# Mean over the rows of an 8192x8192 matrix: four row groups loaded in pairs instead of one by one

## The chip, the cores and the metric

The kernel runs on one core of a Trainium2 chip. The metric is the device time in microseconds, the median over runs; lower is better. The engines that matter here are VectorE (DVE in the profile), TensorE (PE, with PEld for its weight loads), ScalarE (ACT), GpSimd (POOL) and SyncE (SP), which issues the transfers.

## The reference

```python
"x": np.random.randn(8192, 8192).astype(np.float32)

def reference(x):
    return np.mean(x, axis=0)
```

The input is 268.4 MB of float32 in device memory, the output 8192 sums over 8192 rows each, divided by 8192. Every element has to be read once.

## The kernel before

The rows are cut into G = 64 groups of P = 128 rows, one row for each partition. A group is 8192 columns wide, 4 MB, which the kernel counts as 16 blocks of F = 512 columns. The buffer `bufs` holds U = 6 such groups: slots 0 to 3 take the loads, slot 4 is called `both` and slot 5 `acc`, the running sum. The sum over the 128 partitions is made at the end by TensorE, with a column of 1/8192 (`ones`) as the stationary operand. Because a matmul with `ones` can also take a loaded group directly, the last groups are not all added by VectorE.

**The start.** Two small parts of later groups go to a tile of their own (`early`): the last two blocks of group 60, and blocks 9 to 13 of group 63. Groups 0 to 3 come as one load, 4 and 5 as another, and three adds of VectorE make the first `acc` of them.

**The loop of pairs** (line 120), for g = 6, 8, ... 54. One load brings two groups into two neighbouring slots (0 and 1, or 2 and 3, in turn); a partition gets two adjacent rows, 64 KB in one piece. VectorE first adds the two slots into `both`, then adds `both` to `acc`. The slots are free for the next load after the first of the two adds. In two rounds GpSimd adds a part of `early` to `acc` besides.

**The loop of single groups** (line 135), for g = 56 to 59. One load brings one group into one slot, 32 KB for each partition, and VectorE adds the slot to `acc`. The slots are, in this order, 2, 3, 0 and 1.

**The end** (lines 139 to 180). Group 60 comes without its last two blocks, and blocks 0 to 13 of it are added to `acc`. Group 61 comes whole, and VectorE adds blocks 7 to 15 of it to `acc`; TensorE takes blocks 0 to 6 from the buffer. Group 62 is read by TensorE from the buffer, but for blocks 14, 15 and 8, which GpSimd adds to `acc` (line 148). Group 63 comes in four pieces: blocks 4 to 7, 0 to 3, 14 and 15, and 8. Each of these loads goes to the slot of one of the groups 56 to 59: 60 to that of 56, 61 to that of 57, 62 to that of 58 and 63 to that of 59.

**Order and queues.** SyncE issues all loads, in program order. A load waits for the add that frees its slot; at every second load SyncE also waits for two loads that lie six to eight back (`load`, line 75). An add of VectorE that needs a fresh load waits for one no-op, on ScalarE or GpSimd, which in turn waits for that load and for the add before (`add`, line 94). Other adds follow the one before.

**TensorE's order** is written out by hand in the list `sums` (lines 167 to 181), and TensorE keeps to it. Each entry becomes two matmuls in the profile. The sums go to four PSUM tiles: `banks` for blocks 0 to 7, `wide` for 9 to 13, `two` for 14 and 15, `last` for 8. The first entries are blocks 2 to 4 and 0 and 1 of `acc`, blocks 0 to 6 of group 61, blocks 5 to 7 of `acc` and all of group 62's first eight; the last ones belong to the last piece of group 63. ScalarE copies `banks`, `wide` and `two` out of PSUM (line 198), VectorE copies `last` (line 214), and five stores write the output (line 201).

```python
    blocks(acc, 2, 5)
    blocks(acc, 0, 2)
    blocks(r61, 0, 7)
    blocks(acc, 5, 8)
    blocks(r62, 0, 8)
    ...
    spread(two, r63, 14, 16)
    spread(last, r63, 8, 9)
```

Of the kernel before, what the change touches and what calls it, by code (L numbers as in the profile page):

```python
# [9 lines left out]
def kernel(  # L10
# [2 lines left out]
    x: bass.AP,  # L13
    out: bass.AP,
):

    nc = tc.nc
    f32 = mybir.dt.float32
    M, N = x.shape  # L40
# [3 lines left out]
    G = M // P  # L44
# [6 lines left out]
    bufs = sb.tile([P, U, N], f32, name="bufs")  # L51
    both = bufs[:, U - 2, :]
    acc = bufs[:, U - 1, :]
# [21 lines left out]
    def load(dst, src):  # L75
        ins = tc.keep_in_program_order(nc.sync.dma_start(out=dst, in_=src)).ins  # L76
        k = len(loads)
        over = loads[k - 8:k - 6] if k >= 8 and k % 2 == 0 else []
        tc.declare_no_dep(ins, group="loads", keep=over, reason="the reader of the buffer waited")
        for o in over:  # L80
            tc.add_manual_dep(ins, o.name, sync, reason="covers the next load too")
        tc.add_to_no_dep_group("loads", ins)
        loads.append(ins)
        return ins

    def rows(g, n=1):
        return x[g * P:(g + n) * P, :]

    def load_rows(g, u, n):
        return load(bufs[:, u:u + n, :], rows(g, n).rearrange("(p j) c -> p j c", j=n))  # L90
# [3 lines left out]
    def add(dst, a, b, dmas):  # L94

        ins = nc.vector.tensor_add(out=dst, in0=a, in1=b).ins  # L96
        if dmas and adds:
            waiter = nc.scalar if len(adds) % 8 > 1 else nc.gpsimd
            nop = joins[waiter] = tc.keep_in_program_order(waiter.nop()).ins  # L99
            for o in dmas + adds[-1:]:  # L100
                tc.add_manual_dep(nop, o.name, sync, reason="the no-op waits")
            for group in ("loads", "adds"):
                tc.declare_no_dep(ins, group=group, reason="the no-op waited")
            tc.add_manual_dep(ins, nop.name, sync, reason="waits for both at once")
        elif adds:
            tc.declare_no_dep(ins, group="loads", reason="the add ahead waited")
        tc.declare_no_dep(ins, group="early", reason="the no-op waited, or the add behind it")
        tc.add_to_no_dep_group("adds", ins)
        adds.append(ins)
# [7 lines left out]
    tc.keep_in_program_order(nc.scalar.copy(out=warm[:], in_=ones[:]))  # L117
    ahead = []
    g = 6
    while g < G - 8:  # L120
        u = (g + 2) % 4
        dma = load_rows(g, u, 2)
        add(both, bufs[:, u, :], bufs[:, u + 1, :], [dma])
        add(acc, acc, both, ahead)
        ahead = []
        if g in (24, 32):
            lo, hi = (0, 4) if g == 24 else (4, 7)
            cols = slice((9 + lo) * F, (9 + hi) * F)
            ins = tc.keep_in_program_order(nc.gpsimd.tensor_add(  # L129
                out=acc[:, cols], in0=acc[:, cols], in1=early[:, lo * F:hi * F])).ins  # L130
            tc.add_to_no_dep_group("early", ins)
            ahead = [ins]
        g += 2

    while g < G - 4:
        row = bufs[:, (g + 2) % 4, :]
        add(acc, acc, row, [load(row, rows(g))])
        g += 1
    for lo, hi, loaded in [(0, 14, 14), (7, 16, 16)]:
        row = bufs[:, (g + 2) % 4, :]  # L140
        dma = load(row[:, :loaded * F], rows(g)[:, :loaded * F])
# [115 lines left out]
```

## Time and profile before

| | |
|---|---|
| time, median of 3 runs | 628.53 us (628.39 to 628.57) |
| span of the profiled execution | 626.4 us; the page gives no other time for it (the median is 2.13 us longer than this span) |
| VectorE busy | 529.3 us (85% of the span), 60 instructions |
| TensorE busy | 13.3 us (2%), 126 matmuls |
| GpSimd, ScalarE busy | 12.0 us, 3.7 us |
| read from memory | 268.44 MB, 429 GB/s over the span |
| an add of 128x8192 on VectorE | 8763 ns mean of 55; 482.0 us in all |
| VectorE's copy at the end | starts at 623.73 us |

All positions are microseconds from the start of the span. In a line of the timeline the first number is the start and the second the length of a run of like instructions; the bracket at its end says how long the engine was idle before and what released it. In the chain of waits each line is a start, a length and what the time went to. In a group of instructions, the numbers after the bar are busy time, mean ns of one, and the idle time before. In the rows of 40 digits, each digit is the busy share of one fortieth of the span in tenths.

### The profile page before, as it was taken

The numbers are of one execution on the slowest core, as the hardware profiler recorded it, in microseconds if no ns is written. First come the engines' busy times: TensorE is split into PE (matmuls) and PEld (weight loads), VectorE is DVE, ScalarE is ACT, GpSimd is POOL, SyncE is SP. The second block draws the span as 40 slices with busy tenths as digits, with TensorE's granted clock in tenths as the row PEclk, the third lists the DMA queues.
The fourth block names the chain that finished last, engine by engine and source line by source line (L and its number), as shares of the span: only waits on it lengthen the run. The fifth ranks groups of instructions, "written<-read, shape, count | busy, mean of one in ns | idle before, by whom it ended". The sixth has DMA issues, their size and how long they took to land.

```text
span 626.4 us, 484 instructions
## 1 busy us (share of the span) xinstructions
PE 13.3 (2%) x126; PEld 4.0 (1%) x126; DVE 529.3 (85%) x60; ACT 3.7 (1%) x6; POOL 12.0 (2%) x10
## 2 busy tenths in 40 slices
PE   0000000000000000000000000000000000000008
PEld 0000000000000000000000000000000000000002
DVE  0028999998888998889998899888898888999992
ACT  0000000000000000000000000000000000000001
POOL 0000000000000000020000200000000000000002
PEclk9999999999999999999999999999999999999999
DMA  8999999999999999999999999999999999999997
GB/s 372 465 402 428 459 410 460 402 469 402 469 402 469 402 469 402 469 402 469 402 465 406 439 431 427 444 410 460 402 469 402 469 402 469 402 435 435 419 435 305
DMA packets 5930, 268.50 MB, mean 429 GB/s; under 512 B 660, under 2 KB 668, under 8 KB 1064
## 3 DMA queue, kind: packets, MB, share of 16 engines
q1 hardware_dynamic: 5912, 268.46, 99.3%
q8 instruction: 1, 0.02, 0.0%
q10 hardware_dynamic: 16, 0.01, 0.0%
q14 instruction: 1, 0.01, 0.0%
HBM read 268.44 MB, written 0.03 MB: 429 GB/s over the span
## 4 chain that ended last, share of the span: by engine, by line
DMA 59%; DVE 30%; another core or an unknown queue 10%; issue 0%; SPq 0%; ACTq 0%; PE 0%; POOL 0%; POOLq 0%
DMA bufs<-in_x_dram 59%; DVE bufs L96 30%; SPq L76 0%; ACTq L99 0%; PE last L183 0%; DVE tail L214 0%; POOL ready L61 0%; POOL ones L58 0%; POOLq L99 0%; POOLq L241 0%
## 5 line engine op out<-in xcount | busy, mean ns | idle before, releaser
L96 DVE TENSOR_TENSOR bufs<-bufs 128x8192 f32<-128x8192 f32 (+3 forms) x59 | 529.0, 8966 | 85.9 <-DMA bufs<-in_x_dram 43.0
L183 PE MATMUL bank<-bufs,ones 128*32 128x512 f32 x62 | 10.0, 716 | 610.3 <-DVE bufs L96 610.0
L129 POOL TENSOR_TENSOR bufs<-bufs,early 128x2048 f32<-128x2048 f32 (+1 forms) x2 | 7.9, 3954 | 348.5 <-DVE bufs L96 348.5
L148 POOL TENSOR_TENSOR bufs<-bufs 128x1024 f32<-128x1024 f32 (+1 forms) x2 | 3.6, 1824 | 258.9 <-DMA bufs<-in_x_dram 258.9
L214 DVE COPY tail<-last 128x128 f32<-128x128 f32 x1 | 0.3, 291 | 8.8 <-PE last L183 8.8
L183 PEld LDWEIGHTS bank<-bufs,ones 128*32 128x32 f32 x62 | 2.2, 121 | 616.4 <-issue 614.5
L198 ACT COPY bufs<-bank 128x512 f32<-128x512 f32 x2 | 1.2, 586 | 617.9 <-PE bank L183 617.9
L183 PE MATMUL wide<-bufs,ones 128*32 128x512 f32 (+1 forms) x32 | 2.5, 432 | 0.0
L117 ACT ACT_TABLE_LOAD x1 | 1.3, 1283 | 0.7 <-PEq L241 0.7
L183 PE MATMUL two<-bufs,ones 128*32 128x256 f32 x16 | 1.2, 380 | 0.0
L183 PEld LDWEIGHTS wide<-bufs,ones 128*32 128x32 f32 x32 | 1.0, 110 | 1.8 <-issue 1.8
L183 PE MATMUL last<-bufs,ones 128*32 128x128 f32 x16 | 0.8, 279 | 0.1
L198 ACT COPY bufs<-wide 128x640 f32<-128x640 f32 x1 | 0.7, 692 | 1.1 <-PE wide L183 1.1
L183 PEld LDWEIGHTS last<-bufs,ones 128*32 128x32 f32 x16 | 0.4, 109 | 1.2 <-issue 0.6
L183 PEld LDWEIGHTS two<-bufs,ones 128*32 128x32 f32 x16 | 0.4, 109 | 0.1
L198 ACT COPY bufs<-two 128x256 f32<-128x256 f32 x1 | 0.4, 372 | 0.1
L117 ACT COPY warm<-ones 128x32 f32<-128x32 f32 x1 | 0.2, 217 | 0.0
L61 POOL TENSOR_TENSOR ready<-ones 128x1 f32<-128x1 f32 x1 | 0.2, 193 | 0.1
L58 POOL MEMSET ones<- 128x32 f32 x1 | 0.1, 125 | 0.3 <-POOLq L241 0.3
L241 POOL MEMSET const-float32-0.0<- 128x1 f32 x1 | 0.1, 98 | 0.2 <-issue 0.2
L241 POOL MEMSET const-bfloat16-1.0<- 128x1 bf16 x1 | 0.1, 102 | 0.0
L241 POOL MEMSET const-uint8-127<- 128x1 uint8 x1 | 0.1, 102 | 0.0
(1 smaller groups left out, 0.1 us busy)
## 6 DMA issues: line engine op xcount, KB each, us to landing
bufs<-in_x_dram SPq DMA_DIRECT2D x6, 4096.0 KB, 20.4
bufs<-in_x_dram SPq DMA_DIRECT2D x1, 3584.0 KB
bufs<-in_x_dram SPq DMA_DIRECT2D x2, 1024.0 KB, 18.7
early<-in_x_dram SPq DMA_DIRECT2D x1, 1280.0 KB
early<-in_x_dram SPq DMA_DIRECT2D x1, 512.0 KB
bufs<-in_x_dram SPq DMA_DIRECT2D x1, 512.0 KB, 19.4
bufs<-in_x_dram SPq DMA_DIRECT2D x27, 29.9
bufs<-in_x_dram SPq DMA_DIRECT2D x1, 256.0 KB, 19.7
```

Source lines behind the costliest of these rows:

```text
L58: nc.gpsimd.memset(ones[:], 1.0 / M)
L61: nc.gpsimd.tensor_add(out=ready[:], in0=ones[:, 0:1], in1=ones[:, 1:2]))
L96: ins = nc.vector.tensor_add(out=dst, in0=a, in1=b).ins
L117: tc.keep_in_program_order(nc.scalar.copy(out=warm[:], in_=ones[:]))
L129: ins = tc.keep_in_program_order(nc.gpsimd.tensor_add(out=acc[:, cols], in0=acc[:, cols], in1=early[:, lo * F:hi * F])).ins
L148: joined = tc.keep_in_program_order(nc.gpsimd.tensor_add(out=acc[:, cols], in0=acc[:, cols], in1=r62[:, cols])).ins
L183: summed = tc.keep_in_program_order(nc.tensor.matmul(out=dst[32 * q:32 * q + 32, c:c + cols.shape[1]], lhsT=ones[:], rhs=cols, start=all(( ...
L198: return tc.keep_in_program_order(nc.scalar.copy(out=dst, in_=src)).ins
L214: ended = nc.vector.tensor_copy(out=tail[:], in_=last[:]).ins
L241: nc = _bacc.Bacc("TRN2", target_bir_lowering=False, num_devices=1)
```

## The change

Groups 56 to 59 are taken by the loop of pairs, and the loop of single groups goes. Groups 56 and 57 come as one load of 8 MB into slots 2 and 3, groups 58 and 59 as one into slots 0 and 1. VectorE adds the two groups of a pair into `both` and then `both` to `acc`, where before it added each group to `acc`. There are four adds of 128x8192 for these groups in either version. The loads of groups 60 and 61 now both go to slots that the first add of pair 56/57 frees, those of 62 and 63 to slots that the first add of pair 58/59 frees. Empty lines at the head of the function go too, so line numbers in the profile of the changed kernel are smaller by 22 up to the loop and by 26 behind it.

```diff
-    while g < G - 8:
+    while g < G - 4:
         u = (g + 2) % 4
         dma = load_rows(g, u, 2)
         add(both, bufs[:, u, :], bufs[:, u + 1, :], [dma])
...
         g += 2
 
-    while g < G - 4:
-        row = bufs[:, (g + 2) % 4, :]
-        add(acc, acc, row, [load(row, rows(g))])
-        g += 1
     for lo, hi, loaded in [(0, 14, 14), (7, 16, 16)]:
```

## The prediction

> **What bounds the kernel now.** I read the page first, then the chain of waits from 540 us on, the timeline of VectorE, the groups by shape, and the timeline and stretches of the last 15 us. The page says that the transfers are busy from end to end and VectorE 85% of the span:
>
> ```profile
> span 626.4 us, 484 instructions
> DVE  0028999998888998889998899888898888999992
> DMA  8999999999999999999999999999999999999997
> DMA 59%; DVE 30%; another core or an unknown queue 10%; issue 0%; SPq 0%; ACTq 0%; PE 0%; POOL 0%; POOLq 0%
> ```
>
> The profiled span is 626.4 us. The page gives no other time for that execution; the median of the runs shown, 628.53, is 2.13 longer, and I take those 2.13 us around the span as constant.
>
> In the timeline of VectorE every pair of groups is a burst of 17.42 us and a wait of 1.93 us, until 549.50; from there eight adds run without a gap:
>
> ```profile
> 510.81 17.42 DVE L96 TENSOR_TENSOR bufs<-bufs 128x8192 f32<-128x8192 f32 x2 [1.94 <-ACTq L99]
> 530.16 17.42 DVE L96 TENSOR_TENSOR bufs<-bufs 128x8192 f32<-128x8192 f32 x2 [1.93 <-POOLq L99]
> 549.50 65.39 DVE L96 TENSOR_TENSOR bufs<-bufs 128x8192 f32<-128x8192 f32 x8 [1.93 <-ACTq L99]
> 623.73 0.29 DVE L214 COPY tail<-last 128x128 f32<-128x128 f32 x1 [8.83 <-PE last L183]
> ```
>
> So a pair lands every 19.35 us and VectorE needs 17.42 for it: the transfers set the pace (8.39 MB in 19.35 us, 433.5 GB/s). The single loads let VectorE make use of a group when only half a pair is there, and it finishes at 614.89.
>
> The chain of waits shows the end: it goes through the issue of the last loads, their transfer, one matmul group and a copy.
>
> ```profile
> 584.61 8.70 DVE bufs L96
> 593.31 0.02 issue
> ...
> 593.41 8.70 DVE bufs L96
> 602.11 0.02 issue
> ...
> 603.45 19.74 DMA bufs<-in_x_dram
> 623.19 0.04 issue
> 623.23 0.47 PE last L183 x8
> ```
>
> The question is how far TensorE is from being last. The timeline of the last stretch says: not far.
>
> ```profile
> 609.98 6.01 PE L183 MATMUL bank<-bufs,ones 128*32 128x512 f32 x30 [609.98 <-DVE bufs L96]
> 614.95 0.14 PEld L183 LDWEIGHTS bank<-bufs,ones 128*32 128x32 f32 x2 [0.52 <-DVE bufs L96]
> 616.28 0.16 PEld L183 LDWEIGHTS bank<-bufs,ones 128*32 128x32 f32 x8 [1.19 <-DMA bufs<-in_x_dram]
> 616.49 3.61 POOL L148 TENSOR_TENSOR bufs<-bufs 128x1024 f32<-128x1024 f32 x2 [258.93 <-DMA bufs<-in_x_dram]
> 622.54 0.62 PE L183 MATMUL two<-bufs,ones 128*32 128x256 f32 x8
> 623.23 0.16 PEld L183 LDWEIGHTS last<-bufs,ones 128*32 128x32 f32 x8 [0.55 <-DMA bufs<-in_x_dram]
> ```
>
> TensorE starts when the add of group 60 is done (609.98), waits at 614.95 for the add of group 61 (block 7 of the accumulator), waits until 616.28 for group 62, and from then on works through. The starts follow one another without a gap to the eight matmuls at 622.54; those are 256 columns wide, and eight like them that began at 621.03 were followed at 621.46, so they take 0.43 and end their issue at 622.97. Then 0.26 us pass until the last piece of group 63 is there at 623.23. These 0.26 us are all the slack behind 616.28.
>
> **The change part by part.** *Loads.* Four issues of 4 MB become two of 8 MB. The pair 56/57 goes to slots 2 and 3, free when the first add of pair 52 is done; the pair 58/59 to slots 0 and 1, free after the first add of pair 54 (549.50 + 8.70 = 558.2). Those are the moments at which the single loads were free to go, so both pairs travel in the rhythm of the pairs before. Two issues of about 0.35 us go (the issues at 602.13 and 602.50 took 0.33 and 0.43); that is worth nothing, since SyncE sits waiting for VectorE in this stretch. Were SyncE busy, it would be 0.7.
>
> *Adds.* Two adds of 8.70 per pair before and after, so VectorE's work is unchanged. Two of the four joining no-ops go (a no-op and its issues cost about 0.1 us: 593.31 to 593.41); the rows of a pair carry this already. What changes is when the first add may start: when both groups are there. By the rhythm pair 56/57 lands for a start at 549.50 + 19.35 = 568.85. VectorE is through with pair 54 at 566.93 and idles, as in every earlier pair. Pair 58/59 starts at 588.20, and its two adds end at 588.20 + 8.70 + 0.02 + 8.70 = 605.62. Before, the add of group 59 ended at 602.11: **3.51 us later**.
>
> *Loads of 60 to 63.* Group 60 now waits for the first add of pair 56 (568.85 + 8.70 = 577.55, before 575.72), group 61 for the same (before 584.52), 62 and 63 for the first add of pair 58 (596.90; before 593.31 and 602.11). At 596.90 group 61 has still to land: pair 58 lands at 588.15, group 60 takes 7/8 of 9.68, 8.47, to 596.62, and group 61 until 606.30. So the queue has 9.4 us of work when group 62 joins it. The pairs live with less than 11 (each is issued 8.70 after a landing, with 10.65 of the pair ahead left) and their rate doesn't suffer. Cost nothing; the cover is gone only if that issue comes after about 604. The older loads that SyncE also waits for at each second issue lie four to eight loads back and have landed long before.
>
> *Larger pieces.* From the landing of pair 54 (549.44) to that of group 62 (616.24) 66.80 us pass for 28.84 MB; at the rate of the pairs it would be 66.52. All the single loads together thus cost at most 0.28 us, and halving four of them saves 0 to 0.28. I take 0 for the end, because the landing of 588.15 already goes by the pair's own rhythm, and for groups 62 and 63 an earlier landing helps no one who is busy elsewhere. [...]
>
> *Behind the adds.* The two adds on the path have their own rows:
>
> ```profile
> L96 DVE TENSOR_TENSOR bufs<-bufs 128x7168 f32<-128x7168 f32 x1 | 7.6, 7625 | 0.1
> L96 DVE TENSOR_TENSOR bufs<-bufs 128x4608 f32<-128x4608 f32 x1 | 5.0, 4957 | 0.1
> ```
>
> All that hangs on VectorE moves by 3.51: TensorE starts at 613.49, and the add of group 61 ends at 614.89 + 3.51 = 618.40. TensorE's first 28 matmuls are not held by it, the two of block 7 are.
>
> ```profile
> 609.90:613.41 3.51, 3.43 (x16) 0.79 (x17) 3.47 (x1) 0.00 (x0) 0.00 (x0) 1.00 1.04 448
> 618.00:618.86 0.86, 0.86 (x12) 0.18 (x7) 0.00 (x0) 0.00 (x0) 0.86 (x2) 1.00 1.01 419
> ```
>
> In these stretches the second column is TensorE's busy time with its matmuls. The first 16 take 3.43 us, 0.214 each; later eight start in 0.86 (618.02 to 618.88), 0.107 each, although the granted clock reads 1.00 throughout. So 28 matmuls take 3.43 + 12 x 0.107 = 4.71 and are done at 618.20, 0.26 before block 7 may go at 618.46 (0.06 after the add, as at 614.95). Two matmuls more, 0.21: group 62 begins at **618.67 instead of 616.28, 2.39 later**. It has long landed, so the wait for its transfer goes, and what is late next is every matmul behind it. Of the 2.39 the slack takes 0.26, and the last eight matmuls start at 625.36: **+2.13**.
>
> GpSimd's two adds need group 61's add as well: start 0.25 after 618.40, as after the landing of group 62; with 3.61 they end at 622.26. Their readers move by 2.39 to 623.4 and 624.7, so 1 us or more of cover is left even for the later one; without it, each us would count. ScalarE's copies and the stores follow TensorE in the same distances. The copy on VectorE and the last store follow as before.
>
> Sum: 626.4 + 2.13 = 628.53 for the span, and 628.53 + 2.13 = **630.66** for the time, +0.34%.
>
> **The unknown cost is TensorE's slow start.** In the trace it lasts 3.43 us. Shorter gains nothing, as block 7 holds TensorE until 618.46 anyway. Longer costs 0.107 for each matmul that is still slow, less the 0.26. If it lasted twice as long (an estimate, the trace shows one start), the 30 matmuls would end at 613.49 + 6.42 = 619.91 rather than 618.67, and two more would be slow: +1.45, 632.1. Before, this was covered by the wait until 616.28. I take 0, by the one row there is. [...]
>
> **The rivals.** (1) *The slow start is longer*: 630.9 to 632.1. For it: nothing covers it any more. Against it: the one start seen. 0.20. (2) *No difference* (within 0.2%, 1.26 us, about what a measurement can tell): TensorE makes up nearly 0.9 of the 2.13, because the matmuls after 616.28 run closer together once nothing is waited for. Against it: starts at 616.28, 618.02, 618.88, 619.74, 620.60 are 0.107 apart per matmul, gap or no gap. 628.5 to 629.8. 0.10. (3) *Faster*: the larger loads move faster, so that pair 58/59 lands early. Each us of it takes a us off VectorE's end; it decides from 3.4 us on (2.13 + 1.26), that is 9% of the 38.7 us of the two pairs; 4 us would give 626.7. Against it: five pairs in a row at 19.35 with the transfers at their full share. 0.03. (4) *A gap in the transfers* before group 62, as its issue moves from 593.31 to 596.90. One as long as the whole shift, 3.59, moves the last landing from 623.19 to 626.78, past the 625.36 at which TensorE asks for it: 628.53 + 3.59 = 632.1. Up to 2.2 us of gap it would add nothing. Against it: the 9.4 us of queue. 0.03.
>
> **How the numbers follow.** The sum itself, 630.3 to 631.0, has 0.64. Slower by over 0.2% is 0.64 + 0.20 + 0.03 = 0.87, the same 0.10, faster 0.03. For the range I leave out the lower rivals up to their edge and the far end of the slow start: 629.8 to 632.0.
>
> **What would show it.** Right: VectorE's bursts of 17.42 with a wait of about 1.9 also before pairs 56 and 58; a start near 588.2; the last add's end near 618.4; TensorE without the wait for a transfer at group 62 or before its last eight matmuls; the chain ending over VectorE and TensorE, with the last transfer off it. Wrong: pair 58 starting well before 588, or the last matmuls still waiting for the last piece of group 63.

## The result and the profile after

| | before | after |
|---|---|---|
| time, median of 5 runs | 628.57 us (628.39 to 628.81) | 631.51 us (631.24 to 632.17) |
| profiled execution: span | 626.4 us | 629.3 us (time of this run 631.38) |
| last add of VectorE ends | 614.89 | 588.05 + 30.21 = 618.26 |
| TensorE's first matmul | 609.98 | 613.34 |
| VectorE's copy at the end starts | 623.73 | 626.37 |

The change makes the kernel 2.94 us slower. The ratio is 1.005 with a 95% interval of 1.0038 to 1.0063. The forecast was 630.7, within 629.8 to 632.0. The direction and the path were right; 0.8 us of the loss were not in the sum, which had 630.3 to 631.0. The rest of the range was there for a longer slow start of TensorE.

The timeline of VectorE after the change (start, length, what; in the bracket the idle time before):

```profile
549.35 17.42 DVE L74 TENSOR_TENSOR bufs<-bufs 128x8192 f32<-128x8192 f32 x2 [1.93 <-ACTq L77]
568.70 17.42 DVE L74 TENSOR_TENSOR bufs<-bufs 128x8192 f32<-128x8192 f32 x2 [1.93 <-ACTq L77]
588.05 30.21 DVE L74 TENSOR_TENSOR bufs<-bufs 128x8192 f32<-128x8192 f32 x4 [1.93 <-ACTq L77]
626.37 0.29 DVE L188 COPY tail<-last 128x128 f32<-128x128 f32 x1 [8.12 <-PE last L157]
```

The rhythm of burst and wait now goes on through pairs 56/57 and 58/59. Four adds are left behind the last wait, where there were eight before.

The chain of waits after the change (start, length, what):

```profile
588.05 8.70 DVE bufs L74
...
605.57 7.63 DVE bufs L74
613.21 0.14 issue
613.34 7.78 PE bank L157 x45
621.12 0.86 PE wide L157 x8
...
625.64 0.43 PE two L157 x8
626.08 0.27 PE last L157 x5
626.35 0.02 issue
626.37 0.29 DVE tail L188
```

Behind 588 there is no transfer any more. The chain goes over VectorE's adds and then over TensorE to the end, where before it went over the transfer of the last loads.

Of TensorE's timeline, these lines show the slow start (TensorE's first matmuls, at half the later pace: bunches 0.86 us apart against 0.43) and the head of the last stretch:

```profile
616.77 0.19 PEld L157 LDWEIGHTS bank<-bufs,ones 128*32 128x32 f32 x5 [0.68 <-issue]
617.63 0.19 PEld L157 LDWEIGHTS bank<-bufs,ones 128*32 128x32 f32 x3 [0.66 <-issue]
618.31 0.19 PEld L157 LDWEIGHTS bank<-bufs,ones 128*32 128x32 f32 x5 [0.49 <-DVE bufs L74]
618.77 0.16 PEld L157 LDWEIGHTS bank<-bufs,ones 128*32 128x32 f32 x4 [0.27 <-issue]
619.19 1.93 PE L157 MATMUL bank<-bufs,ones 128*32 128x512 f32 x16
...
625.86 0.43 PE L157 MATMUL last<-bufs,ones 128*32 128x128 f32 x8
```

Weight loads come in bunches 0.86 us apart up to 617.63 and some 0.43 us apart from 618.31 on; so the slow start lasted about 4.8 us here, against 3.43 before. The sixteen matmuls at 619.19 are those of group 62. They began at 616.28 before: 2.9 us later, where the prediction had 2.39. The last eight matmuls start at 625.86 instead of 623.23, and they no longer wait for a transfer.

### The profile page after: what moved, and what is told of

The parts are those of the page before. It is cut to its first block, busy times and chain, and to the rows that moved or that the text cites. A ratio compares the mean times of both kernels' runs of the same rounds, so it can differ in the third digit from the quotient of the medians.

```text
span 629.3 us, 478 instructions
## 1 busy us (share of the span) xinstructions
PE 12.9 (2%) x126; PEld 4.9 (1%) x126; DVE 529.3 (84%) x60; ACT 3.7 (1%) x6; POOL 12.0 (2%) x10
## 4 chain that ended last, share of the span: by engine, by line
DMA 61%; DVE 27%; another core or an unknown queue 10%; PE 2%; issue 0%; ACTq 0%; POOL 0%; POOLq 0%
DMA bufs<-in_x_dram 61%; DVE bufs L74 27%; PE bank L157 2%; PE wide L157 0%; PE two L157 0%; ACTq L77 0%; PE last L157 0%; DVE tail L188 0%; POOL ready L39 0%; POOL ones L36 0%; POOLq L77 0%; POOLq L215 0%
## 5 line engine op out<-in xcount | busy, mean ns | idle before, releaser
L172 ACT COPY bufs<-bank 128x512 f32<-128x512 f32 x2 | 1.2, 587 | 620.8 <-PE bank L157 620.8
## 6 DMA issues: line engine op xcount, KB each, us to landing
bufs<-in_x_dram SPq DMA_DIRECT2D x2, 1024.0 KB, 23.3
```

Of the source, the lines that this page charges most:

```text
L172: return tc.keep_in_program_order(nc.scalar.copy(out=dst, in_=src)).ins
```

## The experiments

Three questions were open: whether it is the wait for a pair that costs, and for which pair; where the additional 0.8 us come from; and whether TensorE could take up VectorE's delay. Each kernel was compared with the kernel before on the same chip, so the table gives the difference to that too. None of these kernels leaves out a part of the sum; the additional matmuls go into a PSUM tile that nobody reads. "TensorE made fast ahead" stands for 24 additional matmuls that take the slow start before the first real one; the quarters are those of the columns of TensorE's array, and both are explained below.

| kernel | median, us | above its kernel before, us |
|---|---|---|
| changed kernel | 631.51 | 2.94 |
| groups 58 and 59 as a pair, 56 and 57 one by one | 631.60 | 3.31 |
| groups 56 and 57 as a pair, 58 and 59 one by one | 629.72 | 1.43 |
| single loads, added to each other first | 631.62 | 3.14 |
| pair loads, each group added to the sum | 631.50 | 3.02 |
| changed, TensorE made fast ahead | 631.55 | 3.26 |
| before, TensorE made fast ahead | 629.34 | 1.05, in two sorts of runs |
| changed, one block more in the fourth quarter | 632.38 | 3.90 |
| changed, one block more in the first quarter | 632.47 | 3.99 |
| changed, fast ahead, one block more in the first quarter | 631.64 | 3.13 |
| changed, block 7 of group 61 to TensorE | 630.89 | 2.38 |
| the same, TensorE made fast ahead | 629.57 | 1.06 |

### Which pair, and what of it

Only the last pair (from the kernel before):

```diff
-    while g < G - 4:
+    while g < G - 6:
         row = bufs[:, (g + 2) % 4, :]
         add(acc, acc, row, [load(row, rows(g))])
         g += 1
+    u = (g + 2) % 4
+    dma = load_rows(g, u, 2)
+    add(both, bufs[:, u, :], bufs[:, u + 1, :], [dma])
+    add(acc, acc, both, [])
+    g += 2
```

> Groups 56 and 57 come one by one, 58 and 59 as a pair. Theory: only the landing of the last pair counts; its first add starts at 588.1, the add of group 61 ends at 618.3, and the time is that of the changed kernel, 631.0 to 632.2. Rival (each pair loses its share, through its larger load or through its own wait): about half of the loss, 629.7 to 630.4.

It took 631.60 us, the whole loss. VectorE waits 3.77 us ahead of the pair and starts at 587.92:

```profile
587.92 30.21 DVE L96 TENSOR_TENSOR bufs<-bufs 128x8192 f32<-128x8192 f32 x4 [3.77 <-ACTq L99]
626.15 0.29 DVE L219 COPY tail<-last 128x128 f32<-128x128 f32 x1 [8.02 <-PE last L188]
```

Only the first pair (from the changed kernel, whose loop of pairs ends at `G - 6`; the loop of single groups is put back behind it):

```diff
-    while g < G - 4:
+    while g < G - 6:
...
+    while g < G - 4:
+        row = bufs[:, (g + 2) % 4, :]
+        add(acc, acc, row, [load(row, rows(g))])
+        g += 1
```

> Groups 56 and 57 come as a pair, 58 and 59 one by one. Theory: VectorE idles 1.9 us ahead of pair 56/57, its adds end at 586.1 (before 584.5), and it goes on without a gap, so it is 1.6 us late at the end (616.5 for 614.9). Group 62 lands at 616.2, TensorE begins it 0.2 to 1.0 us late, and of that the slack of 0.26 us goes: 628.5 to 629.3. Rival (each pair loses its share): 629.7 to 630.4.

It took 629.72 us, outside the theory's interval and inside the rival's. Yet the profile shows that VectorE did as the theory had it: 568.85 + 47.80 = 616.65, which is 1.76 us late. What was wrong is the price of a late VectorE. From the timeline of VectorE, and from that of TensorE:

```profile
568.85 47.80 DVE L74 TENSOR_TENSOR bufs<-bufs 128x8192 f32<-128x8192 f32 x6 [1.94 <-ACTq L77]
624.67 0.29 DVE L192 COPY tail<-last 128x128 f32<-128x128 f32 x1 [8.03 <-PE last L161]
```

```profile
616.70 0.26 PEld L161 LDWEIGHTS bank<-bufs,ones 128*32 128x32 f32 x8 [0.74 <-DVE bufs L74]
```

The bracket of the copy at the end is VectorE's idle time since its last add: 8.03 us, and 8.02 in the run with the last pair. In these two profiles TensorE follows VectorE without a wait for a transfer, and the copy comes 8.02 us after the last add. In the kernel before, the last add ended at 614.89, so by this measure TensorE would have been ready for the copy at 622.91, and the copy came at 623.73. VectorE had 0.82 us to spare, not the 1.38 (3.51 less 2.13) that the prediction's sum implies. So the two runs don't split the loss by pairs: in these two the lateness of VectorE's end beyond 0.82 us sets it, 1.76 - 0.82 = 0.94 here, and the copy is 0.94 later than before.

What of a pair costs, its load or its add (both from the kernel before; first, single loads that are added to each other):

```diff
     while g < G - 4:
-        row = bufs[:, (g + 2) % 4, :]
-        add(acc, acc, row, [load(row, rows(g))])
-        g += 1
+        u = (g + 2) % 4
+        dmas = [load(bufs[:, u + j, :], rows(g + j)) for j in range(2)]
+        add(both, bufs[:, u, :], bufs[:, u + 1, :], dmas)
+        add(acc, acc, both, [])
+        g += 2
```

> Groups 56 to 59 come one by one as before, but VectorE adds 56 to 57 and 58 to 59 first, as in the change. Theory: what costs is that VectorE's first add of a pair needs the second group too; group 59 lands near 588, so the time is that of the changed kernel, 631.0 to 632.2. Rival (the larger load as such costs): 628.1 to 628.8.

Second, pair loads whose groups are added to the sum one by one:

```diff
+        u = (g + 2) % 4
+        add(acc, acc, bufs[:, u, :], [load_rows(g, u, 2)])
+        add(acc, acc, bufs[:, u + 1, :], [])
+        g += 2
```

> Groups 56 to 59 come as two loads as in the change, but VectorE adds each group to the accumulator. Theory: a pair's load is done when both groups are there, so VectorE begins at 588 again: 631.0 to 632.2. Rival (the order of the adds is what costs): 628.1 to 628.8.

They took 631.62 and 631.50 us. Either half of the change costs all of it. The adds after pair 58/59 start at 588.36 and 587.96. It is the wait for the second group; the larger load as such neither costs nor helps.

### Where the additional 0.8 us come from

The slow start of TensorE was the first suspect, as the prediction had named it. 24 matmuls were put ahead of TensorE's list, in the changed kernel and in the kernel before:

```diff
+    heat = psp.tile([P, F], f32, name="heat")
...
+    for n in range(24):
+        heated = tc.keep_in_program_order(nc.tensor.matmul(
+            out=heat[32 * (n % 4):32 * (n % 4) + 32, :], lhsT=ones[:], rhs=early[:, :F],
+            start=True, stop=True, tile_position=(0, 32 * (n % 4)), skip_group_check=True,
+        )).ins
+        if n == 0:
+            tc.add_manual_dep(heated, adds[-3].name, sync, reason="starts behind that add")
     for n, (dst, q, c, cols) in enumerate(sums):
```

> The changed kernel with 24 matmuls put ahead of TensorE's list, on data that is long there and into a PSUM tile that nobody reads; they start when the second add of pair 58/59 is done (605.5) and should end about 612.5, before the first real matmul (613.3). Theory (the path is VectorE, then TensorE, and TensorE's slow start of some 4.9 us in the changed kernel costs 0.8 to 0.9 us of it): the matmuls of group 62 begin near 618.5 instead of 619.4, the time falls by about 0.9 to 630.4 to 630.9, and the runs lie closer together than the 0.93 us of the changed kernel. Rival (the part of the loss above 2.13 us lies behind TensorE, in the stores): no change, 631.2 to 632.2. Second rival (the transfers still set the end): no change.

The changed kernel with them took 631.55 us: no gain. The slow start did go: the weight loads of the additional matmuls come about 0.86 us apart up to 609.03, those of the real ones 0.43 apart from 613.80 on. TensorE is through with all that it may do before block 7 and then idles. The lines are weight loads and matmuls of its timeline:

```profile
615.95 0.15 PEld L170 LDWEIGHTS bank<-bufs,ones 128*32 128x32 f32 x3 [0.28 <-issue]
618.39 0.26 PEld L170 LDWEIGHTS bank<-bufs,ones 128*32 128x32 f32 x8 [2.29 <-DVE bufs L75]
618.39 2.33 PE L170 MATMUL bank<-bufs,ones 128*32 128x512 f32 x17 [1.39 <-DVE bufs L75]
```

The end stayed: the copy comes at 626.36, 8.02 after the last add. Only the runs lie closer together, 0.50 us against 0.93, as expected. So the slow start as the sole cause fell, and the suspicion turned to the two matmuls of block 7 themselves. In the trace matmuls start in fours, 0.43 us apart, not one by one every 0.107 us. Each goes to one quarter of the array's columns (`tile_position`, for the blocks 0 to 7 the block's number modulo 4), and the starts fit four quarters side by side, each with 0.43 us for a matmul of its own. Then block 7, alone in the fourth quarter at the head of the last stretch, costs that quarter 0.86 us. To test it, one block more was put behind block 7, into that quarter (3) or into the first (0):

```diff
     blocks(acc, 5, 8)
+    sums.append((heat, 3, 0, early[:, :F]))
```

> The changed kernel with one block more for TensorE (two matmuls of 512 columns, on data that is long there, into a tile that nobody reads), put right behind block 7 of the accumulator and in the same quarter of the array's columns, the fourth. New theory: the four quarters work beside one another at 0.43 us a matmul each, one quarter's matmuls follow one another, and the two of block 7 at the head of the last stretch thus cost 0.86 us rather than 0.21; two more in that quarter cost another 0.86: 632.0 to 632.8. Rival (matmuls follow one another at 0.107 us wherever they go): 0.2 more than the changed kernel, 631.5 to 631.9.

> The same additional block, at the same place in TensorE's order, but in the first quarter of the array's columns. New theory: it runs beside block 7 and costs nothing, 631.2 to 631.8, and the last eight matmuls start within 0.2 us of where the changed kernel has them, about 0.86 us before those of the run with the block in the fourth quarter. Rival (0.107 us a matmul wherever it goes): the same time as with the block in the fourth quarter.

They took 632.38 and 632.47 us. The first agrees: the idle time ahead of the copy is 8.88, 0.86 more than 8.02. The second doesn't: the block wasn't free in the first quarter either. Its profile, of the fastest of its five runs (631.93 us), shows why (weight loads and matmuls of TensorE):

```profile
618.03 0.12 PEld L159 LDWEIGHTS bank<-bufs,ones 128*32 128x32 f32 x3 [0.31 <-issue]
618.33 0.14 PEld L159 LDWEIGHTS bank<-bufs,ones 128*32 128x32 f32 x2 [0.19 <-DVE bufs L75]
618.88 0.59 PE L159 MATMUL heat<-early,ones 128*32 128x512 f32 x1
619.31 0.59 PE L159 MATMUL heat<-early,ones 128*32 128x512 f32 x1
```

The slow start kept the other three quarters at work on the earlier blocks until 618.88, where `heat` begins in the first (they have eight matmuls each up to there, the fourth has six, block 7's two among them). So there are two causes at once, and in the changed kernel they end at about the same time: group 62 begins at 619.19 in one quarter and at 619.24 in the other three. That is also why taking the slow start away gave nothing there.

The slow start isn't of the same length in every execution, though. In the profile of the kernel with single loads added to each other first (a run of 632.09 us, the slowest of its five) it reaches into block 7 itself, whose two matmuls start at 618.62 and 619.48, 0.86 apart. The copy comes 8.58 after the last add there, 0.56 more than 8.02:

```profile
618.62 0.36 PEld L185 LDWEIGHTS bank<-bufs,ones 128*32 128x32 f32 x5 [0.49 <-DVE bufs L96]
619.48 0.22 PEld L185 LDWEIGHTS bank<-bufs,ones 128*32 128x32 f32 x4 [0.50 <-issue]
619.93 0.20 PEld L185 LDWEIGHTS bank<-bufs,ones 128*32 128x32 f32 x4 [0.23 <-issue]
627.15 0.29 DVE L216 COPY tail<-last 128x128 f32<-128x128 f32 x1 [8.58 <-PE last L185]
```

Without the slow start, the block in the first quarter should be free:

> The changed kernel with the 24 matmuls ahead, and with the additional block in the first quarter right behind block 7 of the accumulator. Theory: without the slow start the first quarter is idle while block 7 takes 0.86 us of the fourth, so the block costs 0.1 us at most against the changed kernel with the matmuls ahead (631.55): 631.2 to 631.9. Rival (an additional block costs wherever it stands): 632.1 to 632.6.

It took 631.64 us, against 631.55 without the block. The two quarters start side by side; `bank` at 618.61 is block 7, `spare` the additional block:

```profile
618.61 0.62 PE L172 MATMUL bank<-bufs,ones 128*32 128x512 f32 x1 [1.39 <-DVE bufs L76]
618.62 0.62 PE L172 MATMUL spare<-early,ones 128*32 128x512 f32 x1
618.73 0.93 PE L172 MATMUL bank<-bufs,ones 128*32 128x512 f32 x3
619.07 0.59 PE L172 MATMUL spare<-early,ones 128*32 128x512 f32 x1
```

The second `spare` follows 0.45 after the first, in its own quarter.

### Both causes taken away

Block 7 of group 61 can be left to TensorE, so that none of the blocks 0 to 7 of the sum waits for the last add, with and without the 24 matmuls ahead:

```diff
-    for lo, hi, loaded in [(0, 14, 14), (7, 16, 16)]:
+    for lo, hi, loaded in [(0, 14, 14), (8, 16, 16)]:
...
-    blocks(r61, 0, 7)
+    blocks(r61, 0, 8)
```

> The changed kernel, but VectorE adds only blocks 8 to 15 of group 61 and TensorE takes block 7 of it too, so that no early block of TensorE's list has to wait for the last add. Theory now: two things hold the quarters of the array at the head of the last stretch, and either is enough. The fourth quarter has the two matmuls of block 7 (0.43 us each) from 618.3 on; the other three have eight matmuls each, the first four or more at 0.86 us, and are not through before 619.2. Here the fourth has eight as well and none waits; with a slow start as in the profile of the changed kernel, group 62 begins at 619.2 again: 631.2 to 632.0, with the shortest slow start seen (3.43 us) at 618.5: 630.5. Rival (the wait of block 7 alone costs): 628.7 to 629.5.

> The same, with the 24 matmuls ahead that make TensorE fast before 613.3. Both causes are gone: eight matmuls of 0.43 us in each quarter end at 616.8, group 62 begins there, and VectorE's copy starts at 624.0: 628.7 to 629.3, though VectorE ends 3 us later than in the kernel before. Rival (TensorE can't follow VectorE any faster; its last stretch begins when the last add ends): no less than 630.9.

They took 630.89 and 629.57 us. The first lies between its two cases; the slow start in its profile ended early, between 616.72 and 617.30, and group 62 began at 618.59. The second has group 62 begin at 616.82, a microsecond before the last add ends (588.14 + 29.68 = 617.82), and leaves 1.06 us of the loss. That is short of the 628.7 to 629.3 expected. What is late there is a transfer again:

```profile
622.59 1.07 PE L170 MATMUL bank<-bufs,ones 128*32 128x512 f32 x8 [0.40 <-DMA bufs<-in_x_dram]
...
624.43 0.16 PEld L170 LDWEIGHTS last<-bufs,ones 128*32 128x32 f32 x8 [0.47 <-DMA bufs<-in_x_dram]
...
624.93 0.29 DVE L201 COPY tail<-last 128x128 f32<-128x128 f32 x1 [7.11 <-PE last L170]
```

The pieces of group 63 land late: the profile has 24.8 us from issue to landing for those of 1 MB, 23.3 in the changed kernel. In the list of stretches the last two columns are the busy share of the transfer engines and GB/s; in the changed kernel all is over by 622.5, here a trickle goes on (first the changed kernel, then this one):

```profile
622.50:623.00 0.50, 0.50 (x8) 0.16 (x4) 0.00 (x0) 0.08 (x1) 0.00 (x0) 1.00 0.00 0
```

```profile
622.00:622.50 0.50, 0.19 (x4) 0.00 (x0) 0.00 (x0) 0.24 (x1) 0.00 (x0) 1.00 0.65 234
622.50:623.00 0.50, 0.41 (x4) 0.16 (x8) 0.00 (x0) 0.45 (x1) 0.00 (x0) 1.00 0.06 25
623.00:623.50 0.50, 0.50 (x12) 0.15 (x8) 0.00 (x0) 0.00 (x0) 0.00 (x0) 1.00 0.07 29
623.50:624.00 0.50, 0.50 (x16) 0.26 (x12) 0.00 (x0) 0.28 (x1) 0.00 (x0) 1.00 0.05 20
```

0.06 is about the share of one engine of sixteen, and in the trace's list of packets the last ones of the loads follow one another, one at a time, from 622.38 to 623.96. In this execution a packet of a queue of instructions, 16 KB and 1.09 us long, starts at 619.57, while the loads are under way. It is in the list of queues for 619.4 to 620.8 (packets, MB, share):

```profile
q1 hardware_dynamic: 104, 0.54, 95.8%
q8 instruction: 1, 0.02, 4.9%
```

In the kernel before and in the changed one, the packet of this kind starts at 622.56 and 623.61, when the loads are nearly or wholly through. That this packet is what delays the load is read from the order in time; no run was made without it.

The kernel before with the 24 matmuls showed the same thing from another side:

> The kernel before with the same 24 matmuls, behind the add of group 59 (602.1). Theory: the wait for group 62 at 616.28 covers the slow start and the last piece of group 63 sets the end, so nothing changes: 628.3 to 628.8. Rival (the slow start costs the kernel before too): faster by 0.3 us or more.

Six of its twelve runs took 628.0 to 628.5 us, as the theory had it, the other six 630.2 to 631.0. The profile is of a short run, so one of a long run was wanted:

> The kernel before with the 24 matmuls ahead of TensorE's list, once more: in the first comparison half of its runs took 628.0 to 628.5 us and half 630.2 to 631.0, and the profile was of a short one. Theory: in the long ones a transfer of instructions (16 KB, 1.1 us, one packet) falls into the loads of group 63 and delays a piece of it, as in the run with both measures, where it began at 619.57 instead of 622.56; a profile of a long one should show that packet before 621 and the last piece landing 1 to 2 us after 623.2. Rival (TensorE turns slow again behind its idle time): matmuls 0.86 us apart after 615 and the pieces landing in time. A profile of a short one tells neither.

That run took 630.08 us, and its profile shows TensorE with its work done early and waiting for the last piece of group 63:

```profile
622.25 0.64 PE L196 MATMUL two<-bufs,ones 128*32 128x256 f32 x8
622.95 0.37 ACT L211 COPY bufs<-two 128x256 f32<-128x256 f32 x1
624.30 0.43 PE L196 MATMUL last<-bufs,ones 128*32 128x128 f32 x8 [1.42 <-DMA bufs<-in_x_dram]
```

The last piece lands at 624.26, as expected of a long run, and the matmuls after 615 are in their usual bunches 0.43 us apart, so the rival falls. The packet of instructions wasn't before 621, though: it starts at 622.09 and takes 1.09 us, to 623.18. In the trace's list of packets, two of 2 KB start at 623.16 and 623.38, when all other packets of that piece had started by 622.4. That fits two packets held up behind the 16 KB on one engine. The changed kernel with the matmuls ahead and the additional block shows the same: the packet starts at 622.32 and takes 1.10, one load packet starts at 623.41, when all others had started by 622.56, and the last piece lands at 624.51; TensorE asks for it later there, so it costs nothing. In the short run the packet started at 622.28, and no load packet was held up, so it takes more than its time; that it depends on the engine it falls on was not shown, nor what calls for the packet.

## Why the prediction was right, and where it was off

- *The loads.* Right. The pairs kept the rhythm of 19.35 us (549.35, 568.70, 588.05). Neither a gap before group 62 nor a gain from larger loads showed, and the runs with half of the change each exclude the latter. (The loads that SyncE waits for besides lie seven and eight back by `load`, not four to eight.)
- *The adds.* Right: 3.51 us forecast for VectorE's lateness, 618.26 - 614.89 = 3.37 measured, because the whole profile lies 0.15 us earlier (549.35 for 549.50).
- *The handing over from the transfers to VectorE and TensorE.* Right: the chain of waits has no transfer behind 588.
- *"Two matmuls more, 0.21".* This step failed. The 0.107 us a matmul was the mean over four quarters that work side by side; two matmuls in one quarter take 0.86. That makes 0.65 us. VectorE's time to spare came out 0.56 smaller than the sum implies (0.82 for 1.38); the other 0.09 are not accounted for. The trace of before had it: the two matmuls of block 7 start at 614.95 and 615.40 there. The same mean is in the 4.71 us for the 28 matmuls ahead: three quarters have four fast ones each, and in the trace of before the last of them start at 614.74, 0.43 before they are through, 5.19 after 609.98. By that the 28 would have ended at 613.49 + 5.19 = 618.68, not at 618.20, and still before block 7's quarter was free (618.46 + 0.86 = 619.32).
- *"I take 0" for the slow start.* The row of before said 3.43 us; in the profile of the changed kernel it was about 4.8. Next to block 7 it adds 0.09 there (626.37 - 618.26 = 8.11 instead of 8.02 from the last add to the copy), and 0.56 in the profile where it was longest. It isn't what the sum lacked, as the changed kernel without it is no faster; nor is it nothing, for with block 7 out of the way the kernel took 630.89 us with it and 629.57 without. No run shows the slow start of 4.5 us from which 630.9, the lower edge of rival 1, is worked out. Its length differed more from profile to profile: the shortest slow start (first pair only) ended between 2.6 and 3.2 us after TensorE's first matmul, the longest (single loads added to each other first) between 5.1 and 5.9.
- *The range.* That it holds 631.51 is in part luck. The sum had 630.3 to 631.0, and the range went on to 632.0 for rival 1, the longer slow start. That rival named the right place, but the loss beyond the sum came first from block 7's quarter.
- *The last part.* From the issue of the last store to the end of the span there are 629.3 - 626.69 = 2.61 us, before 626.4 - 624.04 = 2.36. The prediction had the stores follow unchanged. These 0.25 us came in the runs with one pair too (2.61 and 2.63). The two last stores are issued 0.13 apart after the change and 0.41 before; in the two other profiles where they are 0.33 apart it is 2.42 and 2.43. Whether that is the cause was not tried.

The sum by what was measured: 3.37 late on VectorE, less 0.82 to spare, plus 0.09, is 2.64 at the copy; with 0.25 behind it 2.89 for the span (2.9 measured).

The other rivals: the matmuls don't run closer together once nothing is waited for ("no difference"), and the pairs land as the pairs before them ("faster"): the bursts start 19.35 us apart, and no run shows the 4 us less with which that rival comes to 626.7.

## What to carry to other kernels

Near the end of this stream, the size of the last load was a matter of when the next engine may begin: waiting for the second group of the last pair left VectorE 3.4 us late (618.26 for 614.89) with no time behind it to catch up. When the engine that ends last changes, count the new path from its last input by the rows of one execution where it runs unhindered, and not by a mean per instruction over units that work side by side (here 0.21 us for two matmuls that took 0.86). Two causes that end at the same time hide each other: taking one away gained nothing here (the slow start) or 0.6 us (block 7), and only the run without both showed what they cost together.

## What was not expected of the hardware

- The matmuls of the four column quarters come from one list, and yet each quarter kept a time of its own here: a matmul of 512 float32 columns took 0.43 us in each, and 0.86 in the slow start; with the 24 matmuls ahead, block 7 and the additional block began at 618.61 and 618.62.
- The slow start was 3.43 us in one profile, about 4.8 in another and over 5 in a third, with the granted clock shown as 1.00 in all. These are profiles of different kernels; what sets the length was not shown.
- With 24 matmuls more on TensorE, half the runs of the kernel before became about 2 us longer. In the one profile of such a run the last piece of a load landed at 624.26 instead of 623.33 in a short run, although its group 62 was read 0.50 us earlier (615.98 and 616.48).
